# Key-head decays from running sums loaded as rows, and an output projection with both parts side by side

## The chip, the core and the metric

The kernel runs on one core of one Trainium2 chip. A core has a matrix engine (TensorE, PE in the profile, with its weight loads as PEld), a vector engine (VectorE, DVE), an activation engine (ScalarE, ACT), a general engine (GpSimd, POOL) and a queue engine that issues most of the transfers (SyncE, SP). Each engine works through its own instructions in order and waits on semaphores that the others raise. The metric is the device time of one execution in microseconds (us). Lower is better.

## What is computed

A two-layer trunk over 256 latent tokens and 256 context tokens of width 2048. Layer 0 is attention; layer 1 is a chunked gated DeltaNet in both directions. The change lies in layer 1. For each head, direction and chunk of 64 tokens the reference computes

```
gf = jnp.cumsum(gf, axis=-1)
diff = gf[..., :, None] - gf[..., None, :]
decay = jnp.where(lower, jnp.exp(jnp.where(lower, diff, 0.0)), 0.0)
lmat = jnp.where(strict, jnp.einsum('bhncd,bhnsd->bhncs', kb, kf) * decay, 0.0)
...
intra = jnp.where(lower, jnp.einsum('bhncd,bhnsd->bhncs', qf, kf) * decay, 0.0)
```

There `gf` holds the log decays of a chunk, and `kb` the keys times beta. A triangular system with `lmat` is solved per chunk, a recurrence runs over the chunks, and the normalised, gated result goes through the output projection:

```
x = x + gt[:, None] * deltanet_out(o_xf + flip_t(o_xb), zx, o_norm, w_out)
```

and a last RMSNorm. There are 16 key heads, each with 2 value heads.

## The kernel before

**Numbers in two parts.** Activations and weights are split into a high and a low part in a 32-bit matmul format. `split` (lines 74 to 79) casts a block of 1024 weight columns on ScalarE (`whi`, line 77) and subtracts on VectorE (`wlo`, line 78). `dense` (lines 85 to 93) issues three matmuls for each block of 128 rows: high weights by high activations (line 90), high by low (line 91), low by high (line 92). The activations are feature-major tiles `hh` and `hl`, one tag each in the pool `big`; the same two places hold `ch`, `qr` (line 445), `gh`, `gl` of layer 0's output (line 480) and again `hh`, `hl` (line 506). A full unit has 512 columns (latent and context tokens), an `XS` unit the 256 latent ones. Raw weights have four buffers, `whi` and `wlo` three each; SP loads the raw blocks and waits there for a buffer.

**Setup of layer 1 (lines 624 to 675).** One unit gives the betas and log decays. `gst` holds the log decays with tokens on partitions, and `ghl` (lines 661 to 663) their high and low parts. Four matmuls with 0/1 matrices `cum`, `rest`, `hones` give running sums and totals for `neg`, `egm`, `eglb`. The 0/1 matrices `seg` and `incl` come from the constant `dnc`.

**Key heads (`head`, lines 679 to 750).** Each of 16 heads runs a key unit with 512 columns, a query unit with 256, a convolution on VectorE (line 566), transposes to token-major (line 689), then the decays (lines 715 to 725): for three cases (direction 0 with all four tiles, direction 1 with all four, direction 1 with the two latent tiles the other way) GpSimd forms `rhs`, the log decays times `incl`, once for the high and once for the low part (line 720); TensorE multiplies by `seg` (line 722), which sums the log decays between two tokens; ScalarE takes the exponential into `DT` or `DTo` (line 725). `seg` leaves zero in the wrong half, so the exponential is 1 there. Then key by key and key by query products `kk` (line 736), `QKm` (line 740: the query half times the mask `incl`, to SBUF), `NT` (line 744: decay times key products) and `AT` (line 746: decay times `QKm`). The results go to DRAM (lines 749 and 591).

**Inverse (`inverse`, lines 752 to 822).** For each pair of heads VectorE inverts 32-row triangles by 31 steps of two instructions (lines 778 and 780) with stream transposes around them (lines 764, 785, 787), and TensorE joins the halves (lines 798 and 815). The loop of lines 895 to 904 weaves together, per pair of heads, one inverse, two heads and between three and four gate units (`zunits`, 256 columns). PSUM places with the tag `xu` (two) are shared by the decays `pd` and the inverse's `px` and `pu`. The order within each engine is chosen by a planner that simulates a timeline.

**Recurrence and output projection.** From line 1167 to 1255 the order is written by hand. The projection's weights `dn_wo` have 16 output units of 32 blocks of 128 rows. `early` (line 1151) runs the first 24 blocks of units 0 to 7 inside the recurrence's last steps; the loop of line 1264 runs the remaining 8 blocks of those and all 32 of units 8 to 15. The activations are `gh` and `gl` (line 1133), 256 columns each, placed in `hh` and `hl`. `project` (lines 613 to 618) adds the scaled result to the residual, in two VectorE instructions of 128 columns.

Of the kernel before, what the change touches and what calls it, by code (L numbers as in the profile page):

```python
# [8 lines left out]
F32 = mybir.dt.float32  # L9
# [17 lines left out]
def trunk_kernel(ctx: ExitStack, tc: tile.TileContext, g):  # L27
# [57 lines left out]
    def dense(ps, w, off, kt, xh, xl, k0=0, sl=slice(0, T), first=True, last=True):  # L85
        for k in range(kt):
            c = off + k * 128
            wh, wl = w[c // 1024]
            c = slice(c % 1024, c % 1024 + 128)
            PE.matmul(ps, wh[:, c], xh[:, k0 + k, sl], start=first and k == 0, stop=False)  # L90
            PE.matmul(ps, wh[:, c], xl[:, k0 + k, sl], start=False, stop=False)  # L91
            end = PE.matmul(ps, wl[:, c], xh[:, k0 + k, sl], start=False, stop=last and k == kt - 1)  # L92
        return end.ins

    def sliced(wsrc, units, k0, n, xh, xl, pst, first, last):
# [134 lines left out]

    hh = big.tile([128, KT, T], F32R, name="hh", tag="hh")
    hl = big.tile([128, KT, T], F32R, name="hl", tag="hl")
    x1d = scratch("x1d", [128, KT, S])
# [68 lines left out]
    with tc.tile_pool(name="ab", bufs=2, reuse_waits="tile") as tp, \  # L302
# [141 lines left out]
        na7 = na_head(7)  # L444
        ch = big.tile([128, KT, T], F32R, name="ch", tag="hh")
        qr = big.tile([128, KT, T], F32R, name="qr", tag="hl")
        for i, gain in enumerate((q_gain, kv_gain)):
# [31 lines left out]
        pace = 0  # L479
        gh = big.tile([128, KT, T], F32R, name="gh", tag="hh")  # L480
        gl = big.tile([128, KT, T], F32R, name="gl", tag="hl")
        for k in range(KT):
# [22 lines left out]
        rb = rstd_bcast(blocks_of(qacc, sq), 4, D, ps, "st", tp)  # L505
        hh = big.tile([128, KT, T], F32R, name="hh", tag="hh")
        hl = big.tile([128, KT, T], F32R, name="hl", tag="hl")
        modulate(1, lambda k, s: x1[s][:, k], rb, hh, hl, tp)
# [16 lines left out]

    incl = dcst("incl", [128, 3, 64], g["dnc"][:, 1152:1344].rearrange("p (a n) -> p a n", a=3))
    seg = dnp.tile([128, 3, 128], F32R, name="seg", tag="seg")
    taps = dcst("taps", [128, 64, 5], g["taps"])
# [9 lines left out]
    spz = [scratch(f"spz{i}", [128, 2, S]) for i in range(16)]  # L538
    god = scratch("god", [128, 28, S])

    def dunit(u, sl):
# [71 lines left out]
    def project(u, p):  # L613

        for t in range(2):
            x = x_of[u].rearrange("p (c i) -> p c i", c=4)[:, pair(t)]
            V.scalar_tensor_tensor(x, p[:, t * 128:t * 128 + 128].rearrange("p (h i) -> p h i", h=2),
                                   mods[1][:, 32 + u, 0:1], x, op0=ALU.mult, op1=ALU.add)


    with tc.tile_pool(name="dn", bufs=2, reuse_waits="tile") as tp, \
# [9 lines left out]
        qeps = tp.tile([128, 16, 2], F32, name="qeps", tag="qeps", bufs=1)  # L631
        ch = tp.tile([128, 1792], F32, name="cumh", tag="sp", bufs=1)[:, :1152].rearrange("p (a n) -> p a n", a=9)
        nc.sync.dma_start(ch, g["dnc"][:, 0:1152].rearrange("p (a n) -> p a n", a=9))
        cum, rest, hones = ch[:, 0:2], ch[:, 2:4], ch[:, 4:6]
        A.copy(seg, ch[:, 6:9])
        p = dunit(U_BA, FULL)
# [23 lines left out]
        gfl = gst.rearrange("p a k s h -> p a (k s h)")  # L660
        ghl = [tp.tile([128, 2, 128], F32R, name=f"ghl{i}", tag=f"ghl{i}", bufs=1) for i in range(2)]
        A.copy(ghl[0], gfl)
        V.tensor_tensor(ghl[1], gfl, ghl[0].bitcast(F32), op=ALU.subtract)
        for d in range(2):
# [14 lines left out]
        def head(kh):  # L679
# [35 lines left out]
            for d, c, n in ((0, 0, 4), (1, 2, 4), (1, 1, 2)):  # L715
                pd = ps.tile([128, 512], F32, name="pd", tag="xu")[:, :128 * n]
                for i in range(2):
                    rhs = tp.tile([128, 8, 64], F32R, name="rhs", tag="rhs")[:, :2 * n]
                    sh = [128, 2 * n, 64]
                    P.tensor_tensor(rhs, ghl[i].bitcast(F32)[:, d, kh * 8:kh * 8 + 2 * n].unsqueeze(2).broadcast_to(sh),  # L720
                                    incl[:, c].unsqueeze(1).broadcast_to(sh), op=ALU.mult)
                    PE.matmul(pd, seg[:, c], rhs.rearrange("p u i -> p (u i)"), start=i == 0, stop=i == 1)  # L722
                DTs.append(tp.tile([128, n, 2, 64], F32, name="DT", tag="DT") if n == 4 else
                           tp.tile([128, n, 2, 64], F32, name="DTo", tag="DTo", bufs=1))
                A.activation(DTs[-1].rearrange("p s h i -> p (s h i)"), pd, AF.Exp)
            yield
# [3 lines left out]
            for st in range(4):  # L730
                kt = st if st < 2 else st + 2
                for b in range(2):
                    for h in range(2):
# [3 lines left out]
                                  tile_position=(0, r.start))  # L737
            QKm = tp.tile([128, 2, 2, 64], F32, name="QKm", tag="QKm", bufs=1)
            for d in range(2):
                V.tensor_tensor(QKm[:, d], kk[:, 0:2, 64:128], incl[:, d].unsqueeze(1).broadcast_to([128, 2, 64]),  # L740
                                op=ALU.mult)
# [360 lines left out]
        def tile_mm(p, j, k0, xh, xl, sl, first, last):  # L1102

            for k in range(8):
                dense(p, [tuple(wt[j])], 128 * k, 1, xh, xl, k0=k0 + k, sl=sl, first=first and k == 0, last=last and k == 7)
                yield
# [25 lines left out]

        gh, gl = [t.rearrange("p k (a s) -> p (k a) s", a=2) for t in (hh, hl)]

# [16 lines left out]
        def early():  # L1151
            done = None
            for i, (u, c) in enumerate(wo_order):
                if c == 0:
                    p = mm_tile()[:, :S]
                for k, _ in enumerate(tile_mm(p, NV + i, 8 * c, gh, gl, XS, c == 0, c == 2)):
# [107 lines left out]
        for u in [v for e in range(KT - NE) for v in (e, NE + e)]:  # L1264
            k0 = 24 if u < NE else 0
            w = load_split(g["dn_wo"][u][:, 128 * k0:], 4096 - 128 * k0)
            p = (mm_tile() if i % 2 else ps.tile([128, T], F32, name="mm2", tag="ks"))[:, :S]
            dense(p, w, 0, 32 - k0, gh, gl, k0=k0, sl=XS)
            project(u, p)
# [11 lines left out]
def _layout(inputs):  # L1281
# [78 lines left out]
    hon = [np.broadcast_to(h(p) == e, (128, 128)) for e in range(2)]  # L1360
    seg = [(h(p) == h(j)) & m for m in (t(p) > t(j), t(p) < t(j), t(p) >= t(j))]
    inc = [t(p) <= c, t(p) >= c, t(p) < c]
    r["dnc"] = np.concatenate([m.astype(np.float32) for m in cum + rest + hon + seg + inc], 1)
    return r
# [23 lines left out]
```

## Time and profile before

| | us |
|---|---|
| three executions | 2542.07, 2549.25, 2547.64 (median 2547.64) |
| profiled execution | 2550.65 |
| its span, first to last instruction | 2548.9 |

The profile is of the one profiled execution. Busy TensorE time overlaps, since matmuls are pipelined and their ends are modelled; the distance between the starts of two matmuls is the better measure. In a timeline row the first column is the start, the second the duration in us, then engine, line, operation, output and inputs, shape and count; a bracket gives the idle time before it and what ended it. A row of groups has the count, total us, mean ns, idle time before and its releasers.

### The profile page before, as it was taken

What the parts mean: (1) busy time and instruction counts of PE and PEld (TensorE: products, weight loads), DVE (VectorE), ACT (ScalarE), POOL (GpSimd) and SP (SyncE); (2) the same over time, 40 slices, a digit from 0 to 9 for tenths busy, and PEclk for the clock granted to TensorE, in tenths of its full rate; (3) what the DMA queues carried; (4) which work ended last, traced back from release to release, by engine and by line L of the source; (5) the groups of instructions that cost most, each with busy time, mean ns of one, the idle gap of its engine ahead of it and who ended that gap; (6) DMA issues with size and microseconds to landing.
All of it is one profiled execution on the core that took longest, in us unless ns stands there. A gap on an engine that the chain in (4) does not pass through costs nothing.

```text
span 2548.9 us, 43398 instructions
## 1 busy us (share of the span) xinstructions
PE 2448.6 (96%) x16586; PEld 2002.5 (79%) x16586; DVE 1853.5 (73%) x3547; ACT 1140.4 (45%) x2468; POOL 275.6 (11%) x261
## 2 busy tenths in 40 slices
PE   6999999999999999999999989899999999999998
PEld 4557888888768778768888888797777777778898
DVE  4644788873456688758999999997777777777654
ACT  4223323233344422377656665543444444445443
POOL 0000000000000000033322332300000000003000
PEclk9999999999999999999999999999999999999999
DMA  8872645532253367645454544573233333335454
GB/s 251 285 267 83 199 163 172 180 127 91 71 198 112 112 216 225 222 155 160 140 167 148 172 145 156 163 211 104 87 107 110 113 103 105 112 93 180 152 188 141
DMA packets 201809, 394.30 MB, mean 155 GB/s; under 512 B 68224, under 2 KB 109696, under 8 KB 201472
## 3 DMA queue, kind: packets, MB, share of 16 engines
q1 hardware_dynamic: 200448, 389.98, 48.7%
q8 instruction: 131, 2.15, 0.3%
q10 hardware_dynamic: 1152, 1.54, 0.2%
q14 instruction: 78, 0.64, 0.1%
HBM read 356.28 MB, written 35.13 MB: 154 GB/s over the span
## 4 chain that ended last, share of the span: by engine, by line
PE 74%; DVE 12%; issue 6%; DMA 4%; ACT 3%; POOL 0%; SPq 0%; DVEq 0%; POOLq 0%; ACTq 0%
PE mm L90 19%; PE mm L91 17%; PE mm L92 17%; PE pks L993 3%; PE pmod L127 3%; DVE wlo L78 3%; PE ptr L1005 2%; DVE acc L566 2%; PE sp L348 2%; DVE outer L778 1%; PE po L348 1%; DVE X L780 1%; DMA mraw<-dn_wm 1%; DVE U L787 1%; PE ptr L1038 1%
## 5 line engine op out<-in xcount | busy, mean ns | idle before, releaser
L90 PE MATMUL mm<-hh,whi 128*128 128x512 f32 (+1 forms) x2784 | 987.0, 355 | 2.4 <-ACT t L643 2.3
L92 PE MATMUL mm<-hh,wlo 128*128 128x512 f32 (+1 forms) x2784 | 959.3, 345 | 12.2 <-DVE wlo L78 11.5
L91 PE MATMUL mm<-hl,whi 128*128 128x512 f32 (+1 forms) x2784 | 959.7, 345 | 0.0
L77 ACT CAST whi<-raw 128x1024 fp32r<-128x1024 f32 (+2 forms) x346 | 337.6, 980 | 650.5 <-PE mm L91 521.4
L90 PEld LDWEIGHTS mm<-hh,whi 128*128 128x128 f32 x2784 | 534.1, 192 | 112.6 <-issue 33.3
L92 PEld LDWEIGHTS mm<-hh,wlo 128*128 128x128 f32 x2784 | 533.2, 192 | 77.1 <-DVE wlo L78 13.1
L91 PEld LDWEIGHTS mm<-hl,whi 128*128 128x128 f32 x2784 | 534.4, 192 | 62.5 <-issue 9.7
L78 DVE TENSOR_TENSOR wlo<-raw,whi 128x1024 fp32r<-128x1024 f32 (+2 forms) x346 | 400.6, 1160 | 204.0 <-ACT whi L77 201.4
L163 DVE SCALAR_TENSOR_TENSOR lacc<-mraw,cond,lacc 128x512 f32<-128x512 f32 x300 | 208.3, 744 | 0.0
L566 DVE SCALAR_TENSOR_TENSOR acc<-cin,taps,acc 128x508 f32<-128x508 f32 (+3 forms) x256 | 191.9, 750 | 7.6 <-ACT acc L557 5.2
L1015 DVE SCALAR_TENSOR_TENSOR vl<-ptr,egm,vh 128x128 fp32r<-128x128 f32 x224 | 64.6, 346 | 98.2 <-ACT rf L1012 39.3
L720 POOL TENSOR_TENSOR rhs<-ghl,incl 128x512 fp32r<-128x512 f32 (+1 forms) x96 | 113.1, 1193 | 186.6 <-PE pd L722 165.9
L778 DVE SCALAR_TENSOR_TENSOR outer<-L,bv,X 128x31 f32<-128x31 f32 (+15 forms) x248 | 118.1, 476 | 5.1
L127 PE MATMUL pmod<-mraw,cond 128*32 128x512 f32 (+2 forms) x640 | 95.6, 504 | 26.4 <-DMA mraw<-ab_wm 19.1
L1099 DVE TENSOR_TENSOR wlo<-raw,whi 128x1024 fp32r<-128x1024 f32 x84 | 102.5, 1220 | 14.0 <-ACT whi L1091 13.4
L194 POOL TENSOR_TENSOR rs<-ms,half 128x4 f32<-128x4 f32 (+1 forms) x5 | 4.7, 949 | 978.6 <-DVE ms L192 978.6
L580 ACT ACTIVATE ac<-acc 128x128 f32<-128x128 f32 x160 | 37.4, 300 | 153.2 <-DVE acc L566 153.1
L780 DVE TENSOR_TENSOR X<-X,outer 128x31 f32<-128x31 f32 (+15 forms) x248 | 101.1, 408 | 4.9
L90 PE MATMUL mm<-gh,whi 128*128 128x512 f32 x256 | 100.4, 394 | 1.7 <-DVE x1B L498 1.7
L91 PE MATMUL mm<-gl,whi 128*128 128x512 f32 x256 | 100.6, 393 | 0.2 <-DVE gl L486 0.2
L92 PE MATMUL mm<-gh,wlo 128*128 128x512 f32 x256 | 100.1, 392 | 0.0
L1009 ACT ACTIVATE vh<-ptr,egm 128x128 fp32r<-128x128 f32 x224 | 71.2, 374 | 60.7 <-PE ptr L1005 58.9
(290 smaller groups left out, 3562.7 us busy)
## 6 DMA issues: line engine op xcount, KB each, us to landing
raw<-dn_w SPq DMA_DIRECT2D x194, 512.0 KB, 4.1
mraw<-dn_wm SPq DMA_DIRECT2D x96, 512.0 KB, 4.7
mraw<-ab_wm SPq DMA_DIRECT2D x88, 512.0 KB, 5.7
raw<-ab_w SPq DMA_DIRECT2D x66, 512.0 KB, 3.8
raw<-dn_wo SPq DMA_DIRECT2D x64, 512.0 KB, 3.7
raw<-ab_wo SPq DMA_DIRECT2D x32, 512.0 KB, 4.8
raw<-ab_w SPq DMA_DIRECT2D x32, 256.0 KB, 3.5
spt<-sp SPq DMA_DIRECT2D x64, 128.0 KB, 2.2
```

What stands on the lines that cost most here:

```text
L77: A.copy(hi[:, :m], raw[:, :m])
L78: V.tensor_tensor(lo[:, :m], raw[:, :m], hi[:, :m].bitcast(F32), op=ALU.subtract)
L90: PE.matmul(ps, wh[:, c], xh[:, k0 + k, sl], start=first and k == 0, stop=False)
L91: PE.matmul(ps, wh[:, c], xl[:, k0 + k, sl], start=False, stop=False)
L92: end = PE.matmul(ps, wl[:, c], xh[:, k0 + k, sl], start=False, stop=last and k == kt - 1)
L127: PE.matmul(pmod[32 * q:32 * q + 32, :m], cond[:, 4 * kg + q, :], raw[c // 1024][:, half + c % 1024:half + c % 1024 + m], start=kg == 0, s ...
L163: V.scalar_tensor_tensor(acc[:, s], raw[:, q], cond[:, k, s:s + 1], acc[:, s], op0=ALU.mult, op1=ALU.add)
L566: V.scalar_tensor_tensor(o3[:, :, i0:i1], p3[:, :, i0 + d:i1 + d], taps[:, ch, t:t + 1], o3[:, :, i0:i1], op0=ALU.mult, op1=ALU.add)
L720: P.tensor_tensor(rhs, ghl[i].bitcast(F32)[:, d, kh * 8:kh * 8 + 2 * n].unsqueeze(2).broadcast_to(sh), incl[:, c].unsqueeze(1).broadcast_t ...
L778: V.scalar_tensor_tensor(o, L[:, rows, k:k + 1].broadcast_to([128, n, m]), bv[:, k:k + 1], X[:, k:k + 1, cols].broadcast_to([128, n, m]), ...
L780: V.tensor_tensor(X[:, rows, cols], X[:, rows, cols], o, op=ALU.subtract)
L1099: V.tensor_tensor(w, raws[j], h.bitcast(F32), op=ALU.subtract)
```

## The change

Three edits.

**One tile for both parts.** `hh`/`hl`, `ch`/`qr` and `gh`/`gl` become the two halves of one tile `[128, 2, KT, T]` with one tag; their names stay as views.

**Output projection.** A new function `dense2` takes both activation parts as one operand of 512 columns beside each other, so that high by high and high by low are one matmul into two halves of a PSUM tile; low by high stays a matmul of 256 columns. `project` adds both halves to the residual, in four instructions. `early` and the last loop use it, except for the very last unit, which stays as it was.

```
+    def dense2(ps, w, off, kt, x, k0=0, first=True, last=True):
+        p2 = ps.rearrange("p (c s) -> p c s", c=2)
+        for k in range(kt):
...
+            start, stop = first and k == 0, last and k == kt - 1
+            if stop:
+                PE.matmul(p2[:, 0], wl[:, c], x[:, 0, k0 + k], start=False, stop=False)
+            PE.matmul(p2, wh[:, c], x[:, :, k0 + k], start=start, stop=stop)
+            if not stop:
+                PE.matmul(p2[:, 0], wl[:, c], x[:, 0, k0 + k], start=False, stop=False)
```

**Key heads.** In the setup two matmuls (`pgt`) form the running sums with heads on partitions; their high and low parts (`gts`) go to a DRAM scratch `sums`. Per head, `load_sums` reads them back as rows into two operands whose other rows are constant: `grow` (16 rows; two buffers by head parity) and `gcol` (4 rows; one buffer), three transfers for each direction. Each decay is then two matmuls into `pd`: the identity `idr` times `side`, which holds 0 or a very large negative number as the mask, and `grow` times `gcol`, which gives the difference of two running sums. The exponential of a masked place is zero, so `QKm` and its mask go, and `AT` multiplies the decay with `kk` in PSUM.

```
+        def load_sums(kh):
+            for d in range(2):
+                src = sums[d][8 * kh:8 * kh + 8]
+                for h in range(2):
+                    nc.sync.dma_start(grow[d][32:48, kh % 2]...[:, h],
+                                      src.rearrange("u (x h b i) -> (u x) h b i", x=2, h=2, b=2)[:, h])
+                nc.sync.dma_start(gcol[d][0:4].bitcast(F32), src.rearrange("u (r i) -> r u i", r=4))
...
             ack = conv_silu(U_K + kh, FULL, 16 + kh, True)
             yield
+            load_sums(kh)
...
-                for i in range(2):
-                    rhs = tp.tile([128, 8, 64], F32R, name="rhs", tag="rhs")[:, :2 * n]
-                    sh = [128, 2 * n, 64]
-                    P.tensor_tensor(rhs, ghl[i].bitcast(F32)[:, d, kh * 8:kh * 8 + 2 * n].unsqueeze(2).broadcast_to(sh),
-                                    incl[:, c].unsqueeze(1).broadcast_to(sh), op=ALU.mult)
-                    PE.matmul(pd, seg[:, c], rhs.rearrange("p u i -> p (u i)"), start=i == 0, stop=i == 1)
+                PE.matmul(pd, idr, side[:, c].unsqueeze(1).broadcast_to([128, 2 * n, 64]), start=True, stop=False)
+                PE.matmul(pd, grow[d][:, kh % 2], gcol[d][:, :2 * n], start=False, stop=True)
...
-                V.tensor_tensor(QKm[:, d], kk[:, 0:2, 64:128], incl[:, d].unsqueeze(1).broadcast_to([128, 2, 64]),
-                                op=ALU.mult)
...
-                V.tensor_tensor(AT[:, d], DTs[2 * d][:, 0:2], QKm[:, d].unsqueeze(2).broadcast_to([128, 2, 2, 64]),
+                V.tensor_tensor(AT[:, d], DTs[2 * d][:, 0:2], kk[:, 0:2, 64:128].unsqueeze(2).broadcast_to([128, 2, 2, 64]),
                                 op=ALU.mult)
```

On GpSimd the product `rhs` goes; the small root and sum of lines 710 and 711, the memsets of the inverse and its scaling (line 782) stay.

More of the change, by code (lines that the diff above doesn't have):

```diff
@@ L524, in dcst @@
         return t
[L526 to L527 removed]
+    side = dnp.tile([128, 3, 64], F32R, name="side", tag="side")
+    idr = dnp.tile([128, 128], F32R, name="idr", tag="idr")
     taps = dcst("taps", [128, 64, 5], g["taps"])
@@ L539, in trunk_kernel @@
     god = scratch("god", [128, 28, S])
+    sums = [scratch(f"sums{d}", [128, 256]) for d in range(2)]
     def dunit(u, sl):
@@ L660, in trunk_kernel @@
         gfl = gst.rearrange("p a k s h -> p a (k s h)")
-        ghl = [tp.tile([128, 2, 128], F32R, name=f"ghl{i}", tag=f"ghl{i}", bufs=1) for i in range(2)]
-        A.copy(ghl[0], gfl)
-        V.tensor_tensor(ghl[1], gfl, ghl[0].bitcast(F32), op=ALU.subtract)
+        pgt = ps.tile([128, 2, 128], F32, name="pgt", tag="ks")
+        for d in range(2):
+            PE.matmul(pgt[:, d], gfl[:, d], cum[:, d], start=True, stop=True)
+        gts = tp.tile([128, 2, 2, 128], F32R, name="gts", tag="X", bufs=1)
+        gcol = [tp.tile([128, 8, 64], F32R, name=f"gcol{d}", tag="rhs") for d in range(2)]
+        grow = [tp.tile([128, 2, 128], F32R, name=f"grow{d}", tag=f"ghl{d}", bufs=1) for d in range(2)]
+        for d in range(2):
+            A.copy(gts[:, d, 0], pgt[:, d])
+            V.tensor_tensor(gts[:, d, 1], pgt[:, d], gts[:, d, 0].bitcast(F32), op=ALU.subtract)
+            nc.sync.dma_start(sums[d], gts[:, d].bitcast(F32).rearrange("p x n -> p (x n)"))
+            A.copy(gcol[d].rearrange("p u i -> p (u i)"), cons[:, 960:1472])
+            for e in range(2):
+                A.copy(grow[d][:, e], cons[:, 1472:1600])
+        def load_sums(kh):
+            for d in range(2):
+                src = sums[d][8 * kh:8 * kh + 8]
+                for h in range(2):
+                    nc.sync.dma_start(grow[d][32:48, kh % 2].bitcast(F32).rearrange("r (b h i) -> r h b i", b=2, h=2)[:, h],
+                                      src.rearrange("u (x h b i) -> (u x) h b i", x=2, h=2, b=2)[:, h])
+                nc.sync.dma_start(gcol[d][0:4].bitcast(F32), src.rearrange("u (r i) -> r u i", r=4))
         for d in range(2):
@@ L1104, in tile_mm @@
             for k in range(8):
+                if sl is XS:
+                    dense2(p, [tuple(wt[j])], 128 * k, 1, gx, k0=k0 + k, first=first and k == 0, last=last and k == 7)
+                    yield
+                    continue
                 dense(p, [tuple(wt[j])], 128 * k, 1, xh, xl, k0=k0 + k, sl=sl, first=first and k == 0, last=last and k == 7)
@@ L1360, in _layout @@
     hon = [np.broadcast_to(h(p) == e, (128, 128)) for e in range(2)]
-    seg = [(h(p) == h(j)) & m for m in (t(p) > t(j), t(p) < t(j), t(p) >= t(j))]
-    inc = [t(p) <= c, t(p) >= c, t(p) < c]
-    r["dnc"] = np.concatenate([m.astype(np.float32) for m in cum + rest + hon + seg + inc], 1)
+    far = np.float32(1e30)
+    side = [np.where(t(p) > c, -far, 0), np.where(t(p) < c, -far, 0), np.where(t(p) > c, far, 0)]
+    u = np.arange(512)[None, :] // 64
+    cols = np.where((p >= 32) & (p < 48) & ((p - 32) // 2 == u), -1, 0)
+    rows = (p < 4) & (h(j) == p % 2)
+    r["dnc"] = np.concatenate([m.astype(np.float32) for m in cum + rest + hon + side + [cols, rows]], 1)
     return r
```

54 lines of the change are left out of this document (32 added, 22 removed).

## The prediction

> **What bounds the kernel now.** I read the page first: the engines' busy time, their slices, the chain that ended last.
>
> ```profile
> PE 2448.6 (96%) x16586; PEld 2002.5 (79%) x16586; DVE 1853.5 (73%) x3547; ACT 1140.4 (45%) x2468; POOL 275.6 (11%) x261
> ...
> DVE  4644788873456688758999999997777777777654
> ...
> POOL 0000000000000000033322332300000000003000
> ...
> PE 74%; DVE 12%; issue 6%; DMA 4%; ACT 3%; POOL 0%; SPq 0%; DVEq 0%; POOLq 0%; ACTq 0%
> ```
>
> TensorE bounds the whole, but GpSimd works mostly in slices 18 to 26, the key heads, and there VectorE has its nines. So the second view is busy time by stretch (columns: stretch, length, busy us and count of PE, PEld, DVE, ACT, POOL, granted clock, DMA share, GB/s): heads with inverses 0 to 6, the early output projection, the last one.
>
> ```profile
> 1175.00:1690.00 515.00, 475.69 (x4854) 435.98 (x4853) 491.75 (x816) 315.85 (x603) 142.57 (x142) 0.96 0.53 162
> 2325.00:2425.00 100.00, 99.68 (x823) 89.71 (x822) 70.51 (x170) 41.81 (x98) 9.48 (x8) 1.00 0.51 161
> 2425.00:2540.00 115.00, 112.54 (x939) 112.39 (x938) 61.48 (x90) 52.36 (x70) 2.51 (x2) 1.00 0.49 155
> ```
>
> In the heads VectorE is busy 491.75 of 515 us, 95.5%: it is the bound, and TensorE waits for it. In the projection TensorE is. The third view, who waited for whom between 1120 and 1700 (total us, times, longest), says through whom TensorE waits:
>
> ```profile
> POOL rhs L720 <- PE pd L722: 165.9, 43, 18.2
> ...
> ACT ac L577 <- DVE acc L566: 47.0, 10, 7.8
> ...
> PE pd L722 <- ACT U L819: 10.8, 4, 2.8
> ...
> PE mm L92 <- DVE wlo L78: 9.4, 6, 2.6
> ...
> PE pd L722 <- POOL rhs L720: 4.5, 3, 3.8
> ```
>
> TensorE waits little for GpSimd itself (4.5 us); GpSimd waits for TensorE. The removed product matters less by its own wait than by what it does to VectorE.
>
> **The change: what VectorE gets back.** First the groups of one pair of heads with its inverse (1391 to 1466, beside `rhs`), then those of inverse 7 (1690 to 1760, no `rhs` left), then four timeline rows.
>
> ```profile
> L78 DVE TENSOR_TENSOR wlo<-raw,whi 128x1024 fp32r<-128x1024 f32 x16 | 21.5, 1346 | 1.0 <-ACT whi L77 1.0
> L778 DVE SCALAR_TENSOR_TENSOR outer<-L,bv,X 128x31 f32<-128x31 f32 (+15 forms) x31 | 14.0, 452 | 0.6
> L780 DVE TENSOR_TENSOR X<-X,outer 128x31 f32<-128x31 f32 (+15 forms) x31 | 13.6, 440 | 0.7
> ...
> L740 DVE TENSOR_TENSOR QKm<-kk,incl 128x128 f32<-128x128 f32 x4 | 1.0, 278 | 0.0
> ```
>
> ```profile
> L778 DVE SCALAR_TENSOR_TENSOR outer<-L,bv,X 128x31 f32<-128x31 f32 (+15 forms) x31 | 12.4, 400 | 0.8
> L780 DVE TENSOR_TENSOR X<-X,outer 128x31 f32<-128x31 f32 (+15 forms) x31 | 10.6, 342 | 0.9
> ...
> L78 DVE TENSOR_TENSOR wlo<-raw,whi 128x1024 fp32r<-128x1024 f32 x6 | 7.2, 1213 | 0.0
> ```
>
> ```profile
> 1405.82 2.13 POOL L720 TENSOR_TENSOR rhs<-ghl,incl 128x512 fp32r<-128x512 f32 x2 [6.81 <-PE pd L722]
> ...
> 1406.96 2.06 DVE L78 TENSOR_TENSOR wlo<-raw,whi 128x1024 fp32r<-128x1024 f32 x1
> ...
> 1417.79 1.05 POOL L711 TENSOR_TENSOR km<-nrm,root 128x4 f32<-128x4 f32 x1
> ...
> 1417.89 1.21 DVE L78 TENSOR_TENSOR wlo<-raw,whi 128x1024 fp32r<-128x1024 f32 x1
> ```
>
> The same `wlo` takes 2.06 us beside `rhs` and 1.213 alone. The 62 inverse instructions take 27.6 us with `rhs` and 23.0 without: 4.6. The 16 `wlo` lose 16 x (1346 - 1213) ns = 2.1. `QKm` takes 1.0 and goes. That is 7.7 us a pair, and for seven pairs about 53 us, so that VectorE's need falls from 491.75 to 439 us. `AT` keeps its columns and reads PSUM where it read SBUF; I cost that at nothing, as `QKm` read PSUM too at 278 ns for half as many columns.
>
> A rule speaks against counting all of this. The Trainium skill, SBUF — State Buffer, Who interferes with whom, says that a VectorE instruction with two SBUF inputs and a GpSimd instruction that reads SBUF exclude each other for the whole instruction. The lengthened `wlo` beside `rhs` agrees; the 1.21 us `wlo` beside the 1.05 us `km` (line 711), which stays, does not, so I do not count `km` as a blocker.
>
> **What becomes late next: TensorE.** Its need in the same stretch comes from the distance of starts and the counts.
>
> ```profile
> L90 PE MATMUL mm<-hh,whi 128*128 128x256 f32 x693 | 204.2, 295 | 0.0
> ...
> L91 PE MATMUL mm<-hl,whi 128*128 128x512 f32 x200 | 77.9, 390 | 0.0
> ```
>
> ```profile
> 2478.11 0.28 PE L90 MATMUL mm<-hh,whi 128*128 128x256 f32 x1
> ...
> 2478.47 0.28 PE L90 MATMUL mm<-hh,whi 128*128 128x256 f32 x1
> ```
>
> ```profile
> 402.96 0.39 PE L90 MATMUL mm<-hh,whi 128*128 128x512 f32 x1
> ...
> 404.32 0.39 PE L90 MATMUL mm<-hh,whi 128*128 128x512 f32 x1
> ```
>
> ```profile
> 1393.75 2.21 PE L798 MATMUL px<-U,NT 32*32 32x32 f32 x128 [0.57 <-DVE U L787]
> ```
>
> Three matmuls of 256 columns lie 0.36 us apart, 120 ns each; six of 512 columns 1.36 us, 227 ns each. So 3 x 693 x 0.120 = 249.5 and 3 x 200 x 0.227 = 136.2. The 14 heads' decays (four of 512 and two of 256 columns) take 16.1, and are as many after. The 32-wide joins, 768 each of `px` and `pu`, take 2.21 for 128: 26.5 at most. The 32 small `kk` and 8 sums and transposes of a head I put at 0.120 for each of 12 and the rest like `px` (0.55): 14 x 2.0 = 28. Together about 456 us.
>
> So the larger need falls from 491.75 to 456 us. The stage now runs at 95.5% of its larger need; with the same share it takes 456 / 0.955 = 477 us, which is **38 us less**. At the best it is 456 (59 less). At the worst VectorE's relief goes into other in-order waits and nothing is left.
>
> **The output projection.** By the code 192 blocks in `early` and 64 + 224 in the last loop go from three matmuls of 256 columns to one of 512 and one of 256: from 360 to 227 + 120 = 347 ns. 480 x 13 ns = **6.2 us**, all of it on the path, since TensorE is busy 99.68 of 100 and 112.54 of 115 us there. In a sentence by itself: the Trainium skill, TensorE: Matmul & The Clock Gate, Back-to-back issue gap, gives N/2.4 + 2.5 ns, by which the step would go from 327.5 to 325 ns and the sum would be 5 us smaller; the rows above show a fixed part of some 13 ns, so I take the rows.
>
> `project` gets two more instructions in 23 of its 24 calls.
>
> ```profile
> L617 DVE SCALAR_TENSOR_TENSOR xo<-mm,mod,xo x32: 340/343/352, 2330.2 to 2525.4; 128x128 f32<-128x128 f32 x32
> ```
>
> 46 x 0.343 = 16 us of VectorE, under TensorE's work while VectorE is busy 70.51 of 100 and 61.48 of 115 us. Uncovered it would cost these 16 us; the last unit, which ends the kernel, keeps two. I take nothing.
>
> **The new transfers.** Six for each head, on SP's queue, small. The rows for an issue, for four narrow ones, for a landing of 1 KB and of a weight block, and for what SP waits for:
>
> ```profile
> 1409.05 0.35 SPq L71 DMA_DIRECT2D raw<-dn_w  x1
> ...
> 1422.95 1.74 SPq L591 DMA_DIRECT2D spt<-sp  x4
> ```
>
> ```profile
> raw<-dn_w SPq DMA_DIRECT2D x194, 512.0 KB, 4.1
> ...
> ad<-ad SPq DMA_DIRECT2D x1, 1.0 KB, 2.1
> ```
>
> ```profile
> SPq L71 <- DVE wlo L78: 607.4, 170, 12.8
> ```
>
> Six issues take 6 x 0.35 = 2.1 to 6 x 0.44 = 2.6 us of the queue. `gcol` has one buffer, so they wait for the decays of the head before, and weight blocks queue behind them; `wlo`, and through it TensorE, wait for those. But SP waits 607 us for buffers that `wlo` frees: it is mostly early. The bounds are nothing, and one landing of 4.1 us for each of 15 heads, 62 us. I take a tenth of the way, 6 us, since the queue is early and a head has 515 / 14 = 37 us in which to fetch its rows (2.1 us).
>
> **Setup and the joint tile.** More copies on ScalarE (at most 9, of the `gh` size below: under 4 us), a wider constant, one trip through DRAM (two landings of 2.1), all beside the first key unit (48 x 0.227 = 10.9 us); the `rhs` of the first heads goes as well. I take zero, bounds 4 either way. With one tile `gh` can only be written when `qr` too is free. Now `gh` starts early and `gl` waits for `qr`:
>
> ```profile
> 861.09 0.41 ACT L485 CAST gh<-goA 128x256 fp32r<-128x256 f32 x1
> ...
> 878.51 0.41 DVE L486 TENSOR_TENSOR gl<-goA,gh 128x256 fp32r<-128x256 f32 x1
> ```
>
> The second matmul needs `gl` in any case, so the start stays; 32 casts at 0.31 (their distance while they follow each other; taken from 0.41 as an upper size) then run beside the first unit, 16 x 0.68 = 10.9 us. I take 1 us, bounds 0 and 13.
>
> **Sum.** -38 - 6.2 + 6 + 1 = -37 us against the profiled execution's 2550.65 (span 2548.9 and 1.8 around it): 2513.5. That execution lies 3.0 above the median 2547.64, so for a median I say **2510**.
>
> **Rivals.** (a) TensorE's need alone: with slack on both engines the clock dips go too (the heads' granted clock is 0.96, elsewhere 1.00). The heads take 456 us, 21 less than forecast, and the transfers hide: 2510 - 27 = 2483. For it: the waits above are behind VectorE. Chance 0.2. (b) Order, not load, binds: the exponentials and `U` copies stand behind others in ScalarE's queue (10.8 us of `pd <- ACT U`), and only the direct waits on `rhs` and `wlo` (4.5 + 9.4 = 13.9) go. -14 - 6 + 7 = -13: 2535. Chance 0.2. (c) **Slower**: the six transfers hold SP's queue at each head until the decays before have run, and a weight block lands its full 4.1 us late 15 times: 62 us lost, 56 more than I took: 2566. It turns the gain when a head loses more than (38 + 6 - 1) / 15 = 2.9 us. Against it: SP's long waits for `wlo`. Chance 0.07. (d) The two small GpSimd operations that stay (lines 710, 711) block VectorE as `rhs` did, so that the change frees less than it says: 14 heads x 1.05 us more for `km`, 15 us, VectorE's need 454, level with TensorE's. I let half of the 15 us show: 2510 + 8 = 2518. By the skill's rule above this would be so; the 1.21 us `wlo` speaks against it. Chance 0.05. (e) Relief and losses cancel within 0.3%, 2540 to 2555: 0.06.
>
> **How the numbers follow.** The forecast (2495 to 2525) gets the remaining 0.42. A measurement of this kernel can tell some 0.3%, 7.6 us, from no change. Faster: 0.42 + 0.2 + 0.2 + 0.05 = 0.87; same 0.06; slower 0.07. The range leaves out (c), most of (e) and the lower tail of (a): 2480 to 2541.
>
> **What would show it.** Right: in the stretch of the heads VectorE's `wlo` at 1.21 and the 62 inverse instructions at 23 us everywhere; the stretch some 38 us shorter, and TensorE with the larger share. In the projection rows of 512 columns 227 ns before the next. Wrong: TensorE's waits on `wlo` ended by `raw` landings (c), `pd` still waiting for ScalarE (b), or a decay waiting for `gcol`'s transfer.

## The result and the profile after

| | us |
|---|---|
| before, beside the changed kernel | 2548.39 (2542.07 to 2549.25, 4 runs) |
| changed kernel | 2501.87 (2499.32 to 2502.49, 4 runs) |
| ratio, with its 95% interval | 0.982 (0.980 to 0.984) |
| profiled executions, before and after | 2550.65 and 2499.32 |

The change takes 46.5 us off the median, 51.3 between the two profiled executions. The page of the changed kernel, with the lines that answer to those shown of before (busy time, tenths in 40 slices, the chain that ended last):

```profile
PE 2424.6 (97%) x16110; PEld 1961.3 (79%) x16110; DVE 1801.9 (72%) x3562; ACT 1112.0 (45%) x2452; POOL 159.8 (6%) x165
...
DVE  4544778883356687857999999896777777777765
POOL 0000000000000000020001010100000000012000
...
PE 80%; DVE 7%; issue 6%; DMA 3%; ACT 3%; POOL 0%; SPq 0%; DVEq 0%; POOLq 0%; ACTq 0%
```

GpSimd's threes are gone, VectorE's share of the chain falls from 12% to 7% and TensorE's grows from 74% to 80%. Where the 51 us lie is read from four landmarks, in the views of one tile or line (count, duration in ns, start of the first and the last): the first transposition `ptk` of a head, the first `L` of an inverse, the products `ptr<-R` of the recurrence, the last `project`. Before, then after:

```profile
L689 PEld LDWEIGHTS ptk<-ident,ac x64: 138/140/182, 1136.7 to 1632.5; 128*128 128x128 f32 x64
...
L764 DVE STREAM_TRANSPOSE L<-NT x16: 2004/2041/2072, 1172.3 to 1689.8; 64x1024 f32<-64x1024 f32 x16
...
L1005 PE MATMUL ptr<-R,rb x224: 270/275/377, 1791.6 to 2381.6; 128*128 128x128 f32 x112
...
L617 DVE SCALAR_TENSOR_TENSOR xr<-mm,mod,xr x16: 343/347/352, 2435.8 to 2536.9; 128x128 f32<-128x128 f32 x16
```

```profile
L733 PEld LDWEIGHTS ptk<-ident,ac x64: 137/140/143, 1139.4 to 1598.4; 128*128 128x128 f32 x64
...
L800 DVE STREAM_TRANSPOSE L<-NT x16: 1987/2047/2062, 1172.9 to 1643.2; 64x1024 f32<-64x1024 f32 x16
...
L1041 PE MATMUL ptr<-R,rb x224: 270/275/377, 1743.9 to 2332.0; 128*128 128x128 f32 x112
...
L636 DVE SCALAR_TENSOR_TENSOR xr<-mm,mod,xr x30: 341/342/352, 2386.1 to 2485.3; 128x128 f32<-128x128 f32 x30
```

| stretch | before | after | difference |
|---|---|---|---|
| start to first `ptk` | 1136.7 | 1139.4 | +2.7 |
| first `ptk` to first `L` (first heads) | 35.6 | 33.5 | -2.1 |
| first `L` to first `ptr<-R` (other heads, all inverses, the recurrence's first steps) | 619.3 | 571.0 | -48.3 |
| first to last `ptr<-R` (recurrence, early projection) | 590.0 | 588.1 | -1.9 |
| last `ptr<-R` to last `project` (projection) | 155.3 | 153.3 | -2.0 |
| to the end | 12.0 | 12.2 | +0.2 |

Nearly all of it lies in the heads and inverses: from the first to the last `L` it took 517.5 us before and takes 470.3 now, 47.2 less, and from there to the first `ptr<-R` 101.8 and 100.7. The busy time there, inverses 0 to 6 (columns as before), and the groups of one pair (1436 to 1503), after the change:

```profile
1173.00:1641.00 468.00, 452.79 (x4807) 416.82 (x4806) 432.30 (x785) 285.10 (x574) 43.13 (x57) 0.99 0.59 177
```

```profile
L78 DVE TENSOR_TENSOR wlo<-raw,whi 128x1024 fp32r<-128x1024 f32 x16 | 19.5, 1216 | 3.7 <-ACT whi L77 3.5
L814 DVE SCALAR_TENSOR_TENSOR outer<-L,bv,X 128x31 f32<-128x31 f32 (+15 forms) x31 | 12.4, 399 | 0.6
L816 DVE TENSOR_TENSOR X<-X,outer 128x31 f32<-128x31 f32 (+15 forms) x31 | 10.5, 340 | 0.6
```

The 16 `wlo` are back at 1216 ns and the 62 inverse instructions at 22.9 us, where before they took 1346 ns and 27.6 us. VectorE's busy share falls from 95.5% to 432.30 / 468 = 92.4%, TensorE's rises from 92.4% to 452.79 / 468 = 96.7%, and its granted clock from 0.96 to 0.99. By these shares the two have changed places.

### The profile page after: what moved, and what is told of

It is laid out like the page before. It is cut to its first block, busy times and chain, and to the rows that moved or that the text cites. A ratio compares the mean times of both kernels' runs of the same rounds, so it can differ in the third digit from the quotient of the medians.

```text
span 2497.5 us, 42461 instructions
## 1 busy us (share of the span) xinstructions
PE 2424.6 (97%) x16110; PEld 1961.3 (79%) x16110; DVE 1801.9 (72%) x3562; ACT 1112.0 (45%) x2452; POOL 159.8 (6%) x165
## 4 chain that ended last, share of the span: by engine, by line
PE 80%; DVE 7%; issue 6%; DMA 3%; ACT 3%; POOL 0%; SPq 0%; DVEq 0%; POOLq 0%; ACTq 0%
PE mm L90 19%; PE mm L91 18%; PE mm L92 18%; PE pks L1029 3%; PE pmod L141 3%; PE ptr L1041 2%; PE sp L365 2%; PE mm L105 2%; DVE wlo L78 1%; PE po L365 1%; DMA mraw<-dn_wm 1%; PE ptr L1074 1%; PE psu L1060 1%; DMA mraw<-ab_wm 1%; DVE U L823 1%
## 5 line engine op out<-in xcount | busy, mean ns | idle before, releaser
L90 PE MATMUL mm<-hx,whi 128*128 128x512 f32 (+1 forms) x2304 | 843.2, 366 | 2.7 <-ACT t L664 2.2
L91 PE MATMUL mm<-hx,whi 128*128 128x512 f32 (+1 forms) x2304 | 819.5, 356 | 0.0
L92 PE MATMUL mm<-hx,wlo 128*128 128x512 f32 (+1 forms) x2304 | 818.3, 355 | 0.0
L78 DVE TENSOR_TENSOR wlo<-raw,whi 128x1024 fp32r<-128x1024 f32 (+2 forms) x346 | 393.8, 1140 | 207.6 <-ACT whi L77 204.6
L90 PEld LDWEIGHTS mm<-hx,whi 128*128 128x128 f32 x2304 | 438.3, 190 | 105.9 <-issue 27.6
L92 PEld LDWEIGHTS mm<-hx,wlo 128*128 128x128 f32 x2304 | 438.0, 190 | 62.0 <-issue 1.8
L91 PEld LDWEIGHTS mm<-hx,whi 128*128 128x128 f32 x2304 | 438.3, 190 | 61.4 <-issue 8.4
L585 DVE SCALAR_TENSOR_TENSOR acc<-cin,taps,acc 128x508 f32<-128x508 f32 (+3 forms) x256 | 184.1, 719 | 8.0 <-ACT acc L576 5.3
L105 PE MATMUL mm<-hx,whi 128*128 128x512 f32 x480 | 173.1, 404 | 0.3 <-ACT whi L1127 0.3
L107 PE MATMUL mm<-hx,wlo 128*128 128x256 f32 x457 | 128.4, 281 | 1.3 <-DVE wlo L1135 1.3
L105 PEld LDWEIGHTS mm<-hx,whi 128*128 128x128 f32 x480 | 88.9, 188 | 24.6 <-issue 4.6
L90 PE MATMUL mm<-gx,whi 128*128 128x512 f32 x256 | 100.5, 395 | 2.6 <-DVE x1B L515 1.7
L814 DVE SCALAR_TENSOR_TENSOR outer<-L,bv,X 128x31 f32<-128x31 f32 (+15 forms) x248 | 99.1, 400 | 5.2 <-POOL X L809 0.3
L91 PE MATMUL mm<-gx,whi 128*128 128x512 f32 x256 | 100.4, 392 | 0.5 <-DVE gx L503 0.5
L92 PE MATMUL mm<-gx,wlo 128*128 128x512 f32 x256 | 99.8, 391 | 0.0
```

Source lines behind the costliest of these rows:

```text
L78: V.tensor_tensor(lo[:, :m], raw[:, :m], hi[:, :m].bitcast(F32), op=ALU.subtract)
L105: PE.matmul(p2, wh[:, c], x[:, :, k0 + k], start=start, stop=stop)
L107: PE.matmul(p2[:, 0], wl[:, c], x[:, 0, k0 + k], start=False, stop=False)
L585: V.scalar_tensor_tensor(o3[:, :, i0:i1], p3[:, :, i0 + d:i1 + d], taps[:, ch, t:t + 1], o3[:, :, i0:i1], op0=ALU.mult, op1=ALU.add)
L814: V.scalar_tensor_tensor(o, L[:, rows, k:k + 1].broadcast_to([128, n, m]), bv[:, k:k + 1], X[:, k:k + 1, cols].broadcast_to([128, n, m]), ...
```

## The experiments

The theory under test: `rhs` on GpSimd made VectorE's instructions longer, VectorE set the pace of the heads, and the change gains by ending that. The rivals: the gain comes from shorter waits or from GpSimd's amount of work; the transfers or the projection hold a part. Each edit is made to the changed kernel. A time without a ratio is of one execution; times with a ratio are medians of four, beside the kernel before.

**The key heads alone.** Two tiles again and three matmuls for each block of the projection:

```
-    hx = parts_tile("hx")
-    hh, hl = hx[:, 0], hx[:, 1]
+    hh = big.tile([128, KT, T], F32R, name="hh", tag="hh")
+    hl = big.tile([128, KT, T], F32R, name="hl", tag="hl")
...
-            if i < KT - 1:
+            if False:
```

> The key heads changed alone; hh/hl, ch/qr and gh/gl are two tiles again and the projection runs three matmuls of 256 columns. Theory A (the heads carry the gain; the projection is worth 2 us as the trace of after reads, the joint tile costs 1): 2503 us, some 45 below before, heads stretch as in after. Forecast as written (projection 6.2, tile 1): 2507. Rival (the projection and the tile carry a good part through a changed order): above 2515.

Measured: 2504.89 us, ratio 0.982 (0.981 to 0.983); the kernel before took 2550.35 there. The heads alone bring 45.5 us, nearly everything. Its landmarks, in the views of a line:

```profile
L800 DVE STREAM_TRANSPOSE L<-NT x16: 1959/2042/2070, 1171.7 to 1640.4; 64x1024 f32<-64x1024 f32 x16
```

```profile
L1041 PE MATMUL ptr<-R,rb x224: 270/275/377, 1746.3 to 2334.8; 128*128 128x128 f32 x112
```

From first `L` to first `ptr<-R` it takes 574.6 us, 44.7 less than before. The joint tile and the projection together are worth 3.0 us by the two medians, but 1.0 by the two gains, since the kernel before took 2.0 us longer there. Closer than that these runs don't tell.

**GpSimd products back, without a use.** Seven products of 384 columns per head (2688 columns where `rhs` had 2560), of data that lie ready early; nothing reads the result:

```
+                for i in range(3 if n == 4 else 1):
+                    dmy = tp.tile([128, 6, 64], F32, name="dmy", tag="dmy", bufs=1)
+                    sh = [128, 6, 64]
+                    P.tensor_tensor(dmy, gfl[:, d, kh * 8:kh * 8 + 6].unsqueeze(2).broadcast_to(sh),
+                                    ident[:, 0:64].unsqueeze(1).broadcast_to(sh), op=ALU.mult)
```

> The changed kernel with GpSimd products of SBUF operands put back in each head, 7 of 384 columns (2688 beside 2560 before), into a tile that nobody reads. Theory A (the product's SBUF reads lengthen VectorE's two-input instructions, and VectorE was the bound): VectorE gets back some 50 us, the 62 inverse instructions some 27 us a pair again, and the kernel 30 to 45 us slower than after, 2530 to 2545. Rival C (the gain came from the decays no longer waiting for GpSimd, or from a new order): within 5 us of after, 2497 to 2507.

Measured: 2544.18 us, so nearly the whole gain is lost, but not evenly. GpSimd had nothing to wait for and ran all its products at the start. In the windows view, those two stretches and the rest of the heads:

```profile
1144.00:1188.00 44.00, 37.80 (x258) 32.36 (x257) 31.03 (x36) 27.60 (x74) 39.91 (x42) 0.88 0.45 134
1188.00:1276.00 88.00, 71.60 (x480) 65.75 (x479) 86.74 (x110) 39.03 (x83) 64.72 (x68) 0.88 0.36 114
1276.00:1641.00 365.00, 351.47 (x3945) 321.11 (x3944) 339.45 (x602) 215.34 (x439) 44.02 (x56) 0.98 0.57 170
```

The loss sits where GpSimd is busy: VectorE has 86.74 of 88 us there, and TensorE falls to 71.60. The groups of 1188 to 1276 show which instructions grew:

```profile
L819 DVE SCALAR_TENSOR_TENSOR outer<-L,bv,X 128x31 f32<-128x31 f32 (+15 forms) x31 | 22.8, 737 | 0.6
L78 DVE TENSOR_TENSOR wlo<-raw,whi 128x1024 fp32r<-128x1024 f32 x15 | 21.4, 1428 | 0.0
...
L805 DVE STREAM_TRANSPOSE L<-NT 64x1024 f32<-64x1024 f32 x2 | 4.1, 2038 | 0.0
L785 DVE TENSOR_TENSOR NT<-DT,kk 128x512 f32<-128x512 f32 x4 | 2.7, 679 | 0.0
```

`outer` and `wlo`, which read two tensors from SBUF, go from 399 and 1216 to 737 and 1428 ns. The transposition (one input) and `NT` (one of its inputs in PSUM) keep the 2.04 us and 0.68 us that they have without GpSimd's products.

**GpSimd work that reads nothing.** Memsets of the same size, 14 per head:

```
+                for i in range(6 if n == 4 else 2):
+                    dmy = tp.tile([128, 384], F32, name="dmy", tag="dmy", bufs=1)
+                    P.memset(dmy, 0.0)
```

> As the run before, but with 14 GpSimd memsets of 384 columns in each head in place of the products: about the same GpSimd time, written only, nothing read from SBUF. Theory A: no SBUF reads, no lengthening: within 5 us of after, 2497 to 2507, the 62 instructions at 23 us. Rival B (any GpSimd work at the same time holds VectorE): 2530 or more.

Measured: 2499.0 us, no loss. They take GpSimd about as long as the products (224 of some 418 ns, against 112 of some 888), and they too ran early, some before the heads and the others in the same place:

```profile
1172.00:1232.00 60.00, 60.00 (x467) 55.76 (x466) 56.16 (x112) 37.28 (x78) 50.32 (x119) 1.00 0.55 171
```

GpSimd is busy 50.32 of 60 us and the pair takes its 60 us all the same. The groups of this stretch:

```profile
L78 DVE TENSOR_TENSOR wlo<-raw,whi 128x1024 fp32r<-128x1024 f32 x15 | 18.3, 1222 | 2.1 <-ACT whi L77 2.1
L817 DVE SCALAR_TENSOR_TENSOR outer<-L,bv,X 128x31 f32<-128x31 f32 (+15 forms) x31 | 12.4, 400 | 0.6
```

`wlo` and `outer` keep their 1222 and 400 ns. So it is not GpSimd's work that costs, but its reads. The Trainium skill, SBUF — State Buffer, Who interferes with whom, says just this: a VectorE instruction with two SBUF inputs contends with a GpSimd instruction that reads SBUF, not with one that only writes it, and one with at most one SBUF input does not contend, outside the modes that use two ports. These two runs agree in each point.

**The products spread over the heads.** Seven products per head again, but each product reads its own head's keys, so that it can't run ahead:

```
+                    P.tensor_tensor(dmy, sp[:, 0:384], sp[:, 384:768], op=ALU.mult)
```

> As e2 (7 GpSimd products of 384 columns in each head, unread), but they read that head's own keys, so that they can't run ahead of it and are spread over the heads as before the change. Theory A: about 8 us of VectorE a pair come back, a pair of heads with its inverse takes 72 to 75 us where after takes 68, and the kernel 2525 to 2545. Rival C (the steady pairs gained from the new order, and only the crowd of products in e2 hurt): pairs stay at 68, below 2510.

Measured: 2537.37 us (before there 2548.91). Windows view of inverses 0 to 6, and VectorE's groups (1180 to 1685):

```profile
1173.00:1685.00 512.00, 479.10 (x4907) 442.09 (x4906) 489.42 (x796) 285.42 (x581) 167.81 (x158) 0.96 0.54 166
```

```profile
L78 DVE TENSOR_TENSOR wlo<-raw,whi 128x1024 fp32r<-128x1024 f32 x111 | 143.6, 1295 | 13.1 <-ACT whi L77 12.6 <-DMA gcol<-sums 0.4
L817 DVE SCALAR_TENSOR_TENSOR outer<-L,bv,X 128x60 f32<-128x60 f32 (+15 forms) x216 | 104.1, 482 | 4.5
L819 DVE TENSOR_TENSOR X<-X,outer 128x31 f32<-128x31 f32 (+15 forms) x217 | 95.9, 442 | 4.0
```

VectorE's share is 489.42 / 512 = 95.6%, that of the kernel before, the clock is 0.96 again, and 35.5 of the 46.5 us are gone, though nothing waits for these products.

**VectorE's own load.** GpSimd as in the changed kernel, but eight products of 384 columns per head put on VectorE:

```
+                for i in range(3 if n == 4 else 2):
+                    dmy = tp.tile([128, 384], F32, name="dmy", tag="dmy", bufs=1)
+                    V.tensor_tensor(dmy, sp[:, 0:384], sp[:, 384:768], op=ALU.mult)
```

> The changed kernel with VectorE's freed time given back as plain work and GpSimd left idle: 8 products of 384 columns in each head (some 0.5 us each, 8 us a pair), unread. Theory A (VectorE's amount of work was the bound): pairs at 72 to 76 us, the kernel 2525 to 2550. Rival (the order that the planner now finds hides it): below 2512.

Measured: 2548.23 us, the whole gain gone. VectorE's groups, 1175 to 1700:

```profile
L762 DVE TENSOR_TENSOR dmy<-sp 128x384 f32<-128x384 f32 x112 | 61.9, 553 | 3.2 <-ACT sp L752 3.2
```

128 x 0.553 = 70.8 us were added and 46.4 lost. In the quoted stretch 61.9 us were added, and the changed kernel leaves VectorE 468 - 432.30 = 36 us there in which to hide work, so that 26 had to show at the least. Not all of the loss is VectorE's load itself: TensorE's decays now also wait for the rows of `gcol` to land, which they don't in the changed kernel. In the waits view of the same stretch:

```profile
PE pd L765 <- DMA gcol<-sums: 9.0, 6, 2.7
```

**QKm put back** (once multiplied with ones, then read from SBUF by `AT`):

```
+            for d in range(2):
+                V.tensor_tensor(QKm[:, d], kk[:, 0:2, 64:128], ones.rearrange("p (a i) -> p a i", a=2), op=ALU.mult)
...
-                V.tensor_tensor(AT[:, d], DTs[2 * d][:, 0:2], kk[:, 0:2, 64:128].unsqueeze(2)...
+                V.tensor_tensor(AT[:, d], DTs[2 * d][:, 0:2], QKm[:, d].unsqueeze(2)...
```

> The product QKm is put back (VectorE, two instructions of 128 x 128 per head, about 0.27 us each, times ones), and AT reads it from SBUF again; the rest is the changed kernel. Theory (VectorE's spare time is small but there: 432.30 of 468 us in the heads after the change): 1 us a pair of heads of VectorE work comes back, at most 7 to 8 us in all, and most of it is hidden: 2502 to 2506. Rival (VectorE is still the bound of the heads, so each us of its work is a us of the time): 2509 to 2510, 1.0 us x 7.5 pairs slower than the changed kernel. Rival (reading PSUM in AT costs more than reading SBUF, so QKm's going gained nothing): within 1 us of 2502, with AT shorter by as much as QKm costs.

Measured: 2513.72 us, ratio 0.987 (0.985 to 0.988), 11.9 us slower than the changed kernel. None of the three expectations fits: the work is 7.9 us (32 of 283 ns that overlap a little), and `AT` takes as long from SBUF as from PSUM (415 to 417 and 414 ns). In groups (1140 to 1705) and TensorE's timeline:

```profile
L780 DVE TENSOR_TENSOR QKm<-kk,ones 128x128 f32<-128x128 f32 x32 | 7.9, 283 | 0.7 <-PE kk L776 0.7
...
L785 DVE TENSOR_TENSOR sp<-DT,QKm 128x256 f32<-128x256 f32 x16 | 6.7, 417 | 0.0
```

```profile
1709.45 0.76 PE L837 MATMUL px<-U,NT 32*32 32x32 f32 x21 [5.49 <-DVE U L826]
```

So small work on VectorE still shows after the change, though VectorE is idle for 36 us of the heads: the last `L` starts at 1651.9 us, 8.7 later than in the changed kernel, nearest to the expectation that VectorE still binds. Part of the excess behind it is one wait: the last inverse comes late, and TensorE, in its fixed order, stands 5.49 us at the join. That the wait follows from the 7.9 us, and not from the planner's other order, was only argued.

**No transfers.** The rows are loaded for head 0 alone and all heads use its decays:

```
-            load_sums(kh)
+            if kh == 0:
+                load_sums(kh)
...
-                PE.matmul(pd, grow[d][:, kh % 2], gcol[d][:, :2 * n], start=False, stop=True)
+                PE.matmul(pd, grow[d][:, 0], gcol[d][:, :2 * n], start=False, stop=True)
```

> The rows of running sums are loaded once, for the first head, and all heads use them (so the decays are the first head's): 90 of the 96 small transfers are gone. My forecast's term: 6 us faster than after, 2496. Rival: the transfers are hidden, within 2 us of after. If they held back weight blocks at each head: 20 us or more faster.

Measured: 2503.02 us (2500.49 to 2503.99), ratio 0.981 (0.979 to 0.983): without 90 of the 96 transfers the time is the same. In the changed kernel SP does wait for the decays before it may load `gcol` (line 705). In the waits view between 1140 and 1640 this stands beside longer waits for buffers that it has anyway:

```profile
SPq L71 <- DVE outer L814: 56.8, 34, 4.8
...
SPq L705 <- PE pd L761: 22.0, 8, 4.1
```

**Another place for the decays.** `pd` in the PSUM places `ks` instead of `xu`:

```
-                pd = ps.tile([128, 512], F32, name="pd", tag="xu")...
+                pd = ps.tile([128, 512], F32, name="pd", tag="ks")...
```

> The decays' PSUM tile takes the places of tag ks (shared with the transposes ptk) in place of xu (shared with the inverse's joins). In after TensorE waits some 12 us for such a place (rows pd <- ACT U 7.8 and pd <- ACT DT 3.8). If the shared place causes them: 8 to 12 us faster, 2491. Rival (the waits move to ptk or the exponentials): within 3 us, 2499 to 2505, or slower.

Measured: 2505.99 us, ratio 0.984 (0.982 to 0.986), no better. TensorE's waits in the waits view (1120 to 1640), in the changed kernel and in this one:

```profile
PE pd L761 <- ACT U L855: 7.8, 5, 2.1
PE pd L761 <- ACT DT L765: 3.8, 4, 1.3
```

```profile
PE mm L92 <- DVE wlo L78: 3.7, 5, 0.8
PE mm L90 <- ACT whi L77: 3.3, 2, 2.0
PE ptk L733 <- ACT ac L596: 2.5, 3, 1.2
...
PE pd L761 <- ACT DT L765: 2.1, 3, 1.0
```

The wait for ScalarE's `U` goes and others come, and from the first to the last `L` it takes 469.5 us where the changed kernel takes 470.3: what TensorE gains there it waits for again.

**The projection's 512 columns.** In the changed kernel they don't take the 227 ns forecast. TensorE's timeline:

```profile
2440.07 0.28 PE L107 MATMUL mm<-hx,wlo 128*128 128x256 f32 x1
2440.19 0.40 PE L105 MATMUL mm<-hx,whi 128*128 128x512 f32 x1
2440.43 0.28 PE L107 MATMUL mm<-hx,wlo 128*128 128x256 f32 x1
2440.55 0.40 PE L105 MATMUL mm<-hx,whi 128*128 128x512 f32 x1
```

The starts lie 0.36 us apart for both; over 2385 to 2484, where they alternate, the mean is 235.9 ns after one of 512 and 117.1 after one of 256 columns, 353 together. Three edits looked for the cause. First the parts interleaved, so that the 512 columns are one run in SBUF:

```
-        gx = hx.rearrange("p c k (a s) -> p c (k a) s", a=2)
+        gx = hx.rearrange("p c k t -> p (c k t)").rearrange("p (k c s) -> p c k s", c=2, s=S)
```

> Only the place of gh and gl is changed: both parts of a block of rows lie beside each other (512 columns in one run) where in after they lie 32 KB apart. If the two runs cost the 8 ns that a 512-column matmul of the projection takes more than elsewhere (236 against 227): 480 x 8 ns, 3.8 us faster, 2498. Rival (the alternation of 512 and 256 columns costs them): 236 stays, 2502.

The gates of the last steps overwrite here some activations that the last value unit still reads. Measured: 2506.68 us, ratio 0.985 (0.983 to 0.987); the distance stays 236 ns. The few us more come with a wait of 7.7 us for GpSimd's writing of the gates (`gl`, line 1181) in the place that other matmuls still read:

```profile
PEld mm L90 <- POOL hx L1181: 7.7, 1, 7.7
```

Then operand and result given as one run of 512 as well:

```
-            PE.matmul(p2, wh[:, c], x[:, :, k0 + k], start=start, stop=stop)
+            PE.matmul(ps, wh[:, c], xflat[0][:, 512 * (k0 + k):512 * (k0 + k + 1)], start=start, stop=stop)
```

> Both parts of the activations lie interleaved, so that the 512 columns of the wide matmul of the projection are one run, and operand and result are now also given to the instruction as one flat run of 512 instead of 2 x 256. Theory (the two-level address pattern costs the 9 ns between 227 and 236): the 512-column matmuls lie 227 ns before the next again and the tail (2380 to the last projection) is 288 x 9 ns = 2.6 us shorter than in the version with the same placement. Rival (it is the alternation of wide and narrow matmuls with the same weights' fetches, or something else in the stage): 236 as before. As in that version the gates of the last steps overwrite activations that the last value unit still reads.

With the same overwriting as there, measured: the distance stays 236 ns (one execution, 2515.83 us). The address pattern is not the cause. Last, in the final loop, the eight wide matmuls of a weight block in a row and then the eight narrow ones:

```
+        for b in range(0, kt, 8):
+            ks = range(b, min(b + 8, kt))
+            wh, wl = [(k, 0) for k in ks], [(k, 1) for k in ks]
+            if not (last and ks[-1] == kt - 1):
+                seq += wh + wl
```

> In the last loop the eight wide matmuls of a weight block go in a row, then the eight narrow ones (the blocks of early stay alternating). Theory (the alternation of 512 and 256 columns costs the 9 ns): wide matmuls lie 227 ns apart, narrow ones 120, the tail is 288 x 6 ns = 1.7 to 2.6 us shorter than in the changed kernel: about 2500. Rival (the address pattern or the weights' fetch): wide ones keep 235 to 236 ns also next to each other, as the 14 neighbouring ones do in the changed kernel; time as the changed kernel's, 2502, or 1 to 2 us more if the low weights are now late.

Measured: 2499.70 us (2498.77 to 2501.99), ratio 0.981 (0.980 to 0.983). Its timeline, where equal instructions are now joined:

```profile
2439.96 2.23 PE L115 MATMUL mm<-hx,whi 128*128 128x512 f32 x9
2442.03 1.11 PE L113 MATMUL mm<-hx,wlo 128*128 128x256 f32 x8
2442.98 3.36 PE L115 MATMUL mm<-hx,whi 128*128 128x512 f32 x14
```

Nine wide ones take 2442.03 - 2439.96 = 2.07 us, 230 ns each (the first ones 229 to 236, then 226 to 227), eight narrow ones 0.95, 119 each: 349 together. So the alternation costs some 353 - 349 = 4 ns a block, 1.2 us over the 288 blocks of the loop. The median is 2.2 us under the changed kernel's, and the ranges overlap: it has the lowest median here, but these runs can't tell it from the changed kernel.

## Why the prediction was right

The forecast was 2510 us, the time is 2501.87, in the stated range, and the mechanism is the one forecast; sizes were off in three terms.

**VectorE bound the heads through its lengthened instructions: right, but they are not all.** GpSimd's reads put back cost 35.5 and 42.3 us in the two runs, its writes nothing. `QKm` put back costs 11.9 more, where the prediction has it as 1.0 of 7.7 us a pair; no run puts back both.

What VectorE got back is near the forecast 53 us (7 x 7.7 is 54), but in part by luck. In the quoted stretches it is 491.75 - 432.30 = 59 us. By the groups of the whole stretches, `outer` and `X` went from 196.2 to 160.6 us, 36 less where 7 x 4.6 = 32 were counted. `wlo` went from 140.2 to 132.8, 7 less where 7 x 2.1 = 15 were counted, since the pair that the prediction shows has the longest `wlo` of the seven, 1346 ns, and the others lie between 1215 and 1321. `QKm` gave its 6.8. Left out were `acc` (70.0 to 64.8 us) and `AT` (line 746, `sp` in the profile), which was costed at nothing. Before (1175 to 1690) and after (1173 to 1641):

```profile
L746 DVE TENSOR_TENSOR sp<-DT,QKm 128x256 f32<-128x256 f32 x14 | 8.3, 592 | 0.0
```

```profile
L782 DVE TENSOR_TENSOR sp<-DT,kk 128x256 f32<-128x256 f32 x14 | 5.8, 414 | 0.0
```

With both inputs in SBUF the three that met a `rhs` took 1.26 us and the others 0.41, which gives the mean of 592 ns. With one input in PSUM the mean is 414, also beside the spread GpSimd products.

**38 us less in the heads: too small.** From first to last `L` 47.2 us went, in the change as a whole, and 2.1 more in the first heads. The mis-sized step is the share: the forecast let the stage run at 95.5% of the new bound's need, that is 477 us. In the quoted stretches 468 us hold the work, with TensorE busy 96.7% and the clock at 0.99: the share before held TensorE's waits and the dips of its clock, and both were counted as staying. That they go and come together is seen again with the spread products, where VectorE's share is 95.6%, TensorE's 93.6% and the clock 0.96; what each gives was not separated. The need of 456 us was rather high too, since TensorE's busy time in the 468 us is 452.79. Rival (a), where nothing but TensorE's need remains, lay 27 us under the forecast; the truth is 8 under it. The landmarks are those of the two profiled executions, which lie 51.3 us apart, and the medians 46.5, so that each difference here holds a few us that are not the change's.

**The projection, -6.2 us: too large.** 347 ns a block were forecast and 353 measured, so 480 x 7 = 3.4 us; between the last `ptr<-R` and the last `project`, where 288 of the 480 blocks lie, 2.0 show. The step "227 + 120" took the 227 from a row of wide matmuls among wide ones. Here wide and narrow alternate, which costs the wide one 236.

**The transfers, +6 us: nothing.** Without them the time stays. So the waits for the queue cost nothing that shows, and rival (c) with its 62 us falls.

**Setup and joint tile, 0 and +1: not resolved.** The first `ptk` comes at 1139.4 us, 2.7 later than before, and at 1136.9 with two tiles, but between 1136.8 (grouped order) and 1143.1 (flat operands) in other runs with one tile, though these edits change nothing ahead of it. So the setup did not cost much, and more these traces don't say.

**Rivals (b) and (d) fall as well.** `pd` still waits for ScalarE's `U` (7.8 us; 10.8 before), yet the stage gained more than the forecast, so order was not the bound. And the small GpSimd operation `km` doesn't block VectorE for its duration. In the timeline of the changed kernel:

```profile
1496.66 1.09 POOL L755 TENSOR_TENSOR km<-nrm,root 128x4 f32<-128x4 f32 x1
...
1497.16 0.45 DVE L585 SCALAR_TENSOR_TENSOR acc<-cin,taps,acc 128x254 f32<-128x254 f32 x1
...
1497.74 0.48 DVE L585 SCALAR_TENSOR_TENSOR acc<-cin,taps,acc 128x254 f32<-128x254 f32 x1
```

An `acc` inside its 1.09 us takes 0.45, one after it 0.48, and the other VectorE instructions that overlap one of the 16 `km` keep their times as well. So the rule that the two exclude each other for the whole instruction, by which (d) would come about, does not hold for `km`.

## What to carry to other kernels

Look for what an engine does to its neighbours, not only for who waits for it: here TensorE waited 4.5 us for GpSimd directly, and GpSimd's reads cost 35 to 42. Compare the duration of the same instruction beside and without the other engine, multiply by the count, and check that the lengthened engine is the stage's bound. Don't take an engine's idle time for room: in the changed heads VectorE is idle for 36 of 468 us, and yet 7.9 us of work put on it made them end 8.7 us later. When pricing matmuls, take the distance from rows with the same neighbours, and when a bound moves, ask which losses (here TensorE's waits and a lowered clock) may go with it.

## What had not been expected of the hardware

A matmul of 512 columns holds TensorE 236 ns when it alternates with ones of 256, and 227 to 230 in a run of its like; neither where its operand lies nor whether operand and result are one run changes that. The Trainium skill, TensorE: Matmul & The Clock Gate, Back-to-back issue gap, gives a measured sustained 131 ns at 512 columns; no run here comes near it with these 32-bit operands.

Unread GpSimd work that waits for nothing runs ahead as far as it can: 110 instructions crowd into 132 us and do their harm there, so an experiment that puts load back must also put back what paced it.
